# An encoder trunk on one core: the ninth of eleven feed-forward chunks goes from the plain product to the seven-product form in three of four FFNs, split around the first token tile's end

## Chip, core and metric

The kernel runs on 1 core of one Trainium2 chip. What is measured is the device time of one execution in microseconds (us). Five engines work side by side, each through its own list of instructions in order: TensorE (PE, matmuls), VectorE (DVE), ScalarE (ACT), GpSimd (POOL) and SyncE (SP, which issues most DMAs). An engine that needs what another makes waits at a semaphore, and everything behind it in its list waits with it.

## What is computed

Two encoder layers over 256 tokens of width 1024. Each is a macaron block: half a feed-forward network (FFN), a token mixer beside memory attention, half an FFN, each with an RMS norm before and after it.

```python
def swiglu(h, w_gu, w_down):                       # w_gu 1024 x 5632, w_down 2816 x 1024
    g, u = jnp.split(h @ w_gu, 2, axis=-1)
    return (jax.nn.silu(g) * u) @ w_down

for l in range(DEPTH):                             # DEPTH = 2
    ng = norm_gains[l]
    x = x + FFN_RES_WEIGHT * rms_norm(swiglu(rms_norm(x, ng[0]), ffn_w_gu[l, 0], ffn_w_down[l, 0]), ng[1])
    h = rms_norm(x, ng[2])
    ...                                            # l = 0: retention, l = 1: latent attention (MLA)
    x = x + rms_norm(mix, ng[3])
    x = x + FFN_RES_WEIGHT * rms_norm(swiglu(rms_norm(x, ng[4]), ffn_w_gu[l, 1], ffn_w_down[l, 1]), ng[5])
return x
```

There are four FFNs. In the order of time they are called here FFN 1, retention, FFN 2, FFN 3, MLA, FFN 4.

## The kernel before

**Numbers in two halves.** Every matmul is made of three: each operand is split into a high half (`wh`, `zh`, `ah`, cast by ScalarE) and a low half (`wl`, `zl`, `al`, the rest, subtracted by VectorE), and `mm3` adds high x high, low x high and high x low into one PSUM bank (L143 to L145). A `split` therefore always costs one ScalarE and one VectorE instruction of the same size.

**Tiles.** The 256 tokens are two token tiles t = 0, 1 of 128. An FFN walks over 11 chunks c = 0 to 10 of its 2816 inner columns (`FC` = 256 columns each, `C` = 10 is the last). `gu(t, c)` makes gate and up of a chunk (8 blocks of `mm3`, 24 matmuls of 512 columns) into one PSUM bank; `swiglu(t, c)` empties that bank into `a` (ScalarE and VectorE). `a` must be turned before it can be multiplied by the down weights: for chunks 0 to 9 VectorE transposes 32 x 32 blocks (`aT`) and 16 small DMAs (`exchange`, L254) carry the blocks to their places (`ag`); for chunk 10 TensorE transposes it (`tr`).

**Down product, plain.** `down(t, c)` takes 12 matmuls for one token tile, 24 for both.

**Down product, seven-product form.** For chunks below `fast`, `load_fast`, `take_fast` and `down_fast` do both token tiles at once with seven products instead of eight, each of three matmuls (21 in place of 24). Sums and differences of weight blocks (`wB`, three subtractions, five splits) and of activation blocks (`sr`, four additions, three splits) are made for it on VectorE and ScalarE. The seven products accumulate over the chunks in seven PSUM banks (`prod`), and `combine` adds four of them on VectorE into what belongs to all outputs. PSUM has eight banks of 512 f32 columns in this kernel; while the seven products run, one is left for `gu`, `tr` and everything else. `fast` is 5 in FFN 1 and 8 in FFNs 2, 3 and 4.

**Order.** TensorE's list is written out by hand (`manual_schedule`): in the loop over chunks it alternates `gu(0, c)`, half of a seven-product chunk, `gu(1, c)`, the other half. ScalarE's and VectorE's lists, which buffer a tile gets, and the DMAs' order are made by a scheduler from the program, except inside `in_order()` (the first `post`). The end of an FFN is what the change touches: `gu(0, 10)`, the rest of chunks 6 and 7, `combine`, `tr(0, 10)`, the first half of `gu(1, 10)`, `down(0, 8)`, `down(0, 9)`, `down(0, 10)`, the second half of `gu(1, 10)`, then `post(0)` (norm and residual of token tile 0, and the next stage's `z`), `down(1, 8)`, `tr(1, 10)`, the rest of token tile 1, `post(1)`.

The small buffers: `k1` tiles of 256 f32 columns (12 of them), `e` tiles of 512 (5), split weights `wh` and `wl` (9 each), raw weights (5).

Of the kernel before, what the change touches and what calls it, by code (L numbers as in the profile page):

```python
# [31 lines left out]
def kernel(ctx, tc, x, mem, positions, norm_gains, ffn_w_gu, ffn_w_down, w_o,  # L32
                        mem_norm, mem_w_kv, ret_w_in, ret_log_decay, ret_head_norm,
                        mla_w_in, mla_q_norm, mla_kv_norm, mla_w_uq, mla_w_ukv, inv_freq, out):
    nc = tc.nc
    V, S, G, T = nc.vector, nc.scalar, nc.gpsimd, nc.tensor
# [4 lines left out]
    wk = ctx.enter_context(tc.tile_pool(name="wk", bufs=2))  # L41
# [5 lines left out]
    def in_order():  # L47

        return tc.manual_schedule(engines={mybir.EngineType.Activation, mybir.EngineType.DVE})
# [3 lines left out]
        return wk.tile([P, n], dt, name=name, tag="t2", bufs=9)  # L53

    def k1(name, n=256, dt=F32):
        return wk.tile([P, n], dt, name=name, tag="k1", bufs=12)

    def esm(name):
        return wk.tile([P, 512], F32, name=name, tag="e", bufs=5)

    def bank():
        return ps.tile([P, 512], F32, name="bank", tag="bank")
# [199 lines left out]
    def ffn(l, j, zs, gains, extra=(), first=None, fast=0):  # L262
# [5 lines left out]
        sums, prod, gu_last = [[None, None], [None, None]], [], {}  # L268
        extra = dict(extra)
        C = NFC - 1  # L270

        def load_gu(c):
            gu_w[c] = [weights(gu_src(wgu, c, u), 1024) for u in range(KB // 2)]
            gu_last[c] = last_load[0]

        def load_d(c):
            d_w[c] = [weights(wd[c * FC + b * P:c * FC + (b + 1) * P, :], 1024) for b in range(2)]
# [64 lines left out]
                T.matmul(out=prod[p], lhsT=al if x == 2 else ah, rhs=bl if x == 1 else bh,  # L342
                         start=c == 0 and x == 0, stop=x == 2 and c == fast - 1 and not own)

        def combine():

            m1, m5, m7, m6 = prod[0], prod[2], prod[3], prod[6]
            c1, u, v, w = esm("c1"), esm("u"), esm("v"), esm("w")
            S.copy(out=c1, in_=m1)
            add = lambda o, a, b: V.tensor_tensor(out=o, in0=a, in1=b, op=ALU.add)  # L350
            add(u, m6, c1)
            add(v, m5, u)
            add(u, m7, u)
            add(w, m5, u)
            sums[:] = [[c1, v], [u, w]]

        def gu(t, c, part=None):
            if c not in gu_w:
                load_gu(c)
            for k in range(KB) if part is None else range(part * 4, part * 4 + 4):  # L360
                gu_k(t, c, k)
            if part is None:
                swiglu(t, c)

        def gu_k(t, c, k):
# [64 lines left out]
        def down(t, c, hs=(0, 1)):  # L430
            if c not in d_w:
                load_d(c)
            ah, al = at[t, c]
            for i in hs:
                new = accs[t][i] is None
                if new:
                    accs[t][i] = bank()
                for b in range(2):
                    wh, wl = d_w[c][b]
                    n = slice(i * 512, (i + 1) * 512)  # L440
                    m = slice(b * P, (b + 1) * P)
                    mm3(accs[t][i], ah[:, m], al[:, m], wh[:, n], wl[:, n],
                        new and b == 0, c == NFC - 1 and b == 1)
# [5 lines left out]
        def half(c, h):  # L449
            if 0 <= c < fast:  # L450
                down_fast(c, *(range(11, 21) if h else range(11)))
                if h and c == fast - 1:
                    combine()

        if first:
            gu_w[0] = first.w
# [43 lines left out]
            both(C - 3)  # L500
        tr(0, C)
        gu(1, C, 0)
        down(0, C - 2)
        down(0, C - 1)
        down(0, C)
        gu(1, C, 1)
        with in_order():
            z0 = post(0, accs[0], gain_post, True, next_gain, lambda: swiglu(1, C), sums[0])
        down(1, C - 2)
        tr(1, C)  # L510
        down(1, C - 1)
        down(1, C, (0,))
# [719 lines left out]
    zs = [Z(), Z()]  # L1232
# [82 lines left out]
    def mem_extra(m):  # L1315
# [7 lines left out]
        def third():  # L1323
# [6 lines left out]
    late = {7: lambda: (late_mem[7](), angles.append(rope_angles())), 8: lambda: (late_mem[8](), tables()),  # L1330
            9: lambda: (late_mem[9](), tables2())}
    zs = ffn(0, 0, zs, lambda: (gpost(0, 1), gpre(0, 2)), late, first=First(), fast=5)
    zs = retention(zs, m0, lambda: (gpost(0, 3), gpre(0, 4)))
    zs = ffn(0, 1, zs, lambda: (gpost(0, 5), gpre(1, 0)), fast=8)
    m1 = Mem(1, m0.kept)
    zs = ffn(1, 0, zs, lambda: (gpost(1, 1), gpre(1, 2)), {c: lambda i=c - 5: m1.fetch(i) for c in range(5, 9)}, fast=8)
    zs = mla(zs, m1, lambda: (gpost(1, 3), gpre(1, 4)))
    ffn(1, 1, zs, lambda: (gpost(1, 5), None), fast=8)


_INS = ['x', 'mem', 'positions', 'norm_gains', 'ffn_w_gu', 'ffn_w_down', 'w_o', 'mem_norm', 'mem_w_kv',
# [31 lines left out]
```

## Time and profile before

| | us |
|---|---|
| median of 3 runs (lowest to highest) | 945.88 (945.87 to 946.54) |
| the profiled execution's own time | 946.14 |
| its span, first to last instruction | 944.4 |
| PE busy in the span | 929.0 (98%) |
| DVE busy | 787.0 (83%) |
| ACT busy | 589.4 (62%) |

The profile follows one execution. Matmuls are pipelined, so that a matmul's own duration (0.39 us) is longer than the distance to the next one (0.23 us for 512 columns). Where TensorE loses time is read from start to start, and from the waits named behind a row.

### The profile page before, as it was taken

What the parts mean: (1) busy time and instruction counts of PE and PEld (TensorE: products, weight loads), DVE (VectorE), ACT (ScalarE), POOL (GpSimd) and SP (SyncE); (2) the same over time, 40 slices, a digit from 0 to 9 for tenths busy, and PEclk for the clock granted to TensorE, in tenths of its full rate; (3) what the DMA queues carried; (4) which work ended last, traced back from release to release, by engine and by line L of the source; (5) the groups of instructions that cost most, each with busy time, mean ns of one, the idle gap of its engine ahead of it and who ended that gap; (6) DMA issues with size and microseconds to landing.
All of it is one profiled execution on the core that took longest, in us unless ns stands there. A gap on an engine that the chain in (4) does not pass through costs nothing.

```text
span 944.4 us, 13761 instructions
## 1 busy us (share of the span) xinstructions
PE 929.0 (98%) x4400; PEld 772.0 (82%) x4400; DVE 787.0 (83%) x1341; ACT 589.4 (62%) x1030; POOL 179.0 (19%) x328
## 2 busy tenths in 40 slices
PE   9999999999999999999999999999999999999996
PEld 7878878898888888888887878888897888888885
DVE  6989979587886788999988699999766887999994
ACT  7656665456665565666656467676568864666761
POOL 0331231030000114033101332031020013330210
PEclk9999999999999999999999999999999999999998
DMA  9966478684655575767457967855551759667531
GB/s 314 336 219 217 142 239 268 207 278 140 198 170 182 153 257 195 247 223 239 144 158 224 326 196 240 264 184 192 169 187 44 246 157 301 190 199 236 170 133 45
DMA packets 152537, 194.25 MB, mean 206 GB/s; under 512 B 15112, under 2 KB 126224, under 8 KB 152464
## 3 DMA queue, kind: packets, MB, share of 16 engines
q1 hardware_dynamic: 143232, 183.92, 60.4%
q0 software_dynamic: 9216, 9.46, 3.3%
q8 instruction: 34, 0.56, 0.2%
q14 instruction: 39, 0.32, 0.1%
q10 hardware_dynamic: 16, 0.00, 0.0%
HBM read 179.69 MB, written 3.15 MB: 194 GB/s over the span
## 4 chain that ended last, share of the span: by engine, by line
PE 81%; DMA 7%; DVE 5%; ACT 3%; issue 2%; POOL 1%; SPq 1%; DVEq 0%; POOLq 0%; ACTq 0%
PE bank L145 21%; PE bank L143 21%; PE bank L144 21%; PE bank L342 14%; DMA raw<-in_ffn_w_gu_dram 3%; DMA ag<-aT 3%; PE bank L173 2%; DVE wl L77 2%; ACT wh L76 1%; POOL ag L254 1%; PE bank L643 1%; PE bank L898 1%; DVE x L241 1%; PE bank L884 1%; ACT e L654 0%
## 5 line engine op out<-in xcount | busy, mean ns | idle before, releaser
L143 PE MATMUL bank<-wh,zh 128*128 128x512 f32 (+2 forms) x944 | 364.6, 386 | 0.0
L144 PE MATMUL bank<-wl,zh 128*128 128x512 f32 (+2 forms) x944 | 360.5, 382 | 1.1 <-DVE wl L77 1.1
L145 PE MATMUL bank<-wh,zl 128*128 128x512 f32 (+2 forms) x944 | 360.5, 382 | 0.4 <-DVE zl L77 0.4
L77 DVE TENSOR_TENSOR wl<-raw,wh 128x1024 fp32r<-128x1024 f32 (+2 forms) x262 | 311.1, 1210 | 34.7 <-ACT wh L76 32.0
L76 ACT CAST wh<-raw 128x1024 fp32r<-128x1024 f32 (+2 forms) x262 | 269.8, 1045 | 65.3 <-PE bank L145 19.4
L254 POOL DMA_DIRECT2D ag<-aT x288 | 141.3, 498 | 393.3 <-ACT sh L76 280.1
L144 PEld LDWEIGHTS bank<-wl,zh 128*128 128x128 f32 x944 | 177.9, 188 | 35.2 <-DVE wl L77 1.8
L145 PEld LDWEIGHTS bank<-wh,zl 128*128 128x128 f32 x944 | 177.5, 188 | 35.3 <-DVE zl L77 1.0
L143 PEld LDWEIGHTS bank<-wh,zh 128*128 128x128 f32 x944 | 177.8, 188 | 33.4 <-issue 0.7
L76 ACT CAST wh<-wB 128x1024 fp32r<-128x1024 f32 (+1 forms) x116 | 94.4, 836 | 75.0 <-DVE wB L297 39.5
L77 DVE TENSOR_TENSOR wl<-wB,wh 128x1024 fp32r<-128x1024 f32 (+1 forms) x116 | 108.0, 952 | 11.6 <-ACT wh L76 10.4
L377 ACT ACTIVATE s<-bank,rstd 128x256 f32<-128x256 f32 x88 | 41.6, 472 | 48.3 <-PE bank L145 44.8
L143 PE MATMUL bank<-wh,ah 128*128 128x512 f32 x120 | 47.6, 396 | 0.0
L148 POOL TENSOR_TENSOR prs<-ms,nhalf 128x1 f32<-128x1 f32 x12 | 10.1, 843 | 194.0 <-DVE ms L161 194.0
L145 PE MATMUL bank<-wh,al 128*128 128x512 f32 x120 | 46.9, 390 | 0.0
L144 PE MATMUL bank<-wl,ah 128*128 128x512 f32 x120 | 46.7, 390 | 0.0
L76 ACT CAST ah<-ag 128x256 fp32r<-128x256 f32 x80 | 25.2, 368 | 18.1 <-DMA ag<-aT 16.0
L401 DVE STREAM_TRANSPOSE aT<-a 128x256 f32<-128x256 f32 x80 | 35.4, 443 | 0.9
L148 POOL TENSOR_TENSOR rstd<-ms,nhalf 128x1 f32<-128x1 f32 x14 | 21.2, 1518 | 78.6 <-DVE ms L161 78.6
L342 PE MATMUL bank<-wh,sl 128*128 128x512 f32 x87 | 34.6, 398 | 1.4 <-DVE sl L77 1.4
L76 ACT CAST sh<-sr 128x512 fp32r<-128x512 f32 x29 | 18.0, 621 | 28.2 <-DVE sr L318 28.2
L342 PE MATMUL bank<-wh,sh 128*128 128x512 f32 x87 | 34.5, 397 | 1.0 <-ACT sh L76 1.0
(213 smaller groups left out, 1164.1 us busy)
## 6 DMA issues: line engine op xcount, KB each, us to landing
raw<-in_ffn_w_gu_dram SPq DMA_DIRECT2D x352, 256.0 KB, 4.6
raw<-in_ffn_w_down_dram SPq DMA_DIRECT2D x30, 512.0 KB, 4.8
wB<-in_ffn_w_down_dram SPq DMA_DIRECT2D x58, 256.0 KB, 4.6
wB<-in_ffn_w_down_dram SPq DMA_DIRECT2D x29, 512.0 KB, 4.0
raw<-in_ret_w_in_dram SPq DMA_DIRECT2D x48, 256.0 KB, 4.1
ag<-aT POOLq DMA_DIRECT2D x288, 32.0 KB, 3.6
raw<-in_w_o_dram SPq DMA_DIRECT2D x16, 512.0 KB, 4.0
raw<-in_mem_w_kv_dram SPq DMA_DIRECT2D x8, 512.0 KB, 5.4
```

The lines of the kernel that those rows point to most:

```text
L76: ins = S.copy(out=hi, in_=src).ins
L77: V.tensor_tensor(out=lo, in0=src, in1=hi.bitcast(F32), op=ALU.subtract)
L143: T.matmul(out=dst, lhsT=ah, rhs=bh, start=start, stop=False)
L144: T.matmul(out=dst, lhsT=ah, rhs=bl, start=False, stop=False)
L145: T.matmul(out=dst, lhsT=al, rhs=bh, start=False, stop=stop)
L148: G.tensor_tensor(out=dst, in0=src, in1=nhalf.broadcast_to(list(src.shape)), op=ALU.pow)
L173: T.transpose(out=tp[:s.shape[1], j * P:(j + 1) * P], in_=s, identity=ident)
L241: V.scalar_tensor_tensor(out=xx[:, sl], in0=y[i][:, sl], scalar=r, in1=xx[:, sl], op0=ALU.mult, op1=ALU.add)
L254: queues[q % len(queues)].dma_start(out=g[q * 32:(q + 1) * 32, i * 256:(i + 1) * 256], in_=b[sl, q * 256:(q + 1) * 256])
L342: T.matmul(out=prod[p], lhsT=al if x == 2 else ah, rhs=bl if x == 1 else bh, start=c == 0 and x == 0, stop=x == 2 and c == fast - 1 and no ...
L377: s_ins = S.activation(out=s, in_=p[:, 0:FC], func=AF.Silu, scale=z.r).ins
L401: V.transpose(out=b.rearrange("p (q u t b x) -> p u t q b x", q=4, u=2, t=2, b=2)[:, c % 2, t], in_=act.pop((t, c)).rearrange("p (b q x) - ...
```

## The change

In FFNs 2, 3 and 4 `fast` becomes 9, so that chunk 8 is made with seven products. Its 21 matmuls are not done in one go: products 0, 6, 2, 4 and 1 (15 matmuls), which token tile 0 needs, stand where `down(0, 8)` (12) stood, and products 3 and 5 (6 matmuls) where `down(1, 8)` (12) stood. `combine` is cut in two, one part behind each. GpSimd's space for DMA descriptors goes from 1024 to 2048 bytes per partition, and `k1` gives up one of its 12 buffers for it. FFN 1 keeps its form.

```diff
-        return wk.tile([P, n], dt, name=name, tag="k1", bufs=12)
+        return wk.tile([P, n], dt, name=name, tag="k1", bufs=11)
...
-        def combine():
+        def add(o, a, b):
+            V.tensor_tensor(out=o, in0=a, in1=b, op=ALU.add)
+
+        def combine(t):
             m1, m5, m7, m6 = prod[0], prod[2], prod[3], prod[6]
-            c1, u, v, w = esm("c1"), esm("u"), esm("v"), esm("w")
-            S.copy(out=c1, in_=m1)
-            add = lambda o, a, b: V.tensor_tensor(out=o, in0=a, in1=b, op=ALU.add)
-            add(u, m6, c1)
-            add(v, m5, u)
-            add(u, m7, u)
-            add(w, m5, u)
-            sums[:] = [[c1, v], [u, w]]
+            if t == 0:
+                c, u, v = esm("c"), esm("u"), esm("v")
+                S.copy(out=c, in_=m1)
+                add(u, m6, c)
+                add(v, m5, u)
+                sums[:] = [[c, v], [u, esm("w")]]
+            else:
+                u, w = sums[1]
+                add(u, m7, u)
+                add(w, m5, u)
...
                 if h and c == fast - 1:
-                    combine()
+                    combine(0)
+                    combine(1)
...
         tr(0, C)
         gu(1, C, 0)
-        down(0, C - 2)
+        late = C - 2 == fast - 1
+        if late:
+            down_fast(C - 2, *(3 * p + x for p in (0, 6, 2, 4, 1) for x in range(3)))
+            combine(0)
+        else:
+            down(0, C - 2)
         down(0, C - 1)
         down(0, C)
         gu(1, C, 1)
+        if late:
+            down_fast(C - 2, *(3 * p + x for p in (3, 5) for x in range(3)))
         with in_order():
             z0 = post(0, accs[0], gain_post, True, next_gain, lambda: swiglu(1, C), sums[0])
-        down(1, C - 2)
+        if late:
+            combine(1)
+        else:
+            down(1, C - 2)
         tr(1, C)
...
-    zs = ffn(0, 1, zs, lambda: (gpost(0, 5), gpre(1, 0)), fast=8)
+    zs = ffn(0, 1, zs, lambda: (gpost(0, 5), gpre(1, 0)), fast=9)
...
-    nc = _bacc.Bacc("TRN2", target_bir_lowering=False, num_devices=1, dynamic_dma_scratch_size=1024)
+    nc = _bacc.Bacc("TRN2", target_bir_lowering=False, num_devices=1, dynamic_dma_scratch_size=2048)
```

Three places in the engines' lists, all of FFN 2's end. The number behind a name tells buffers apart.

TensorE, before: the end of chunk 7 (L342), the two transposes of `tr(0, 10)` into `bank_5031`, and the start of the first half of `gu(1, 10)` into `bank_5036`; in brackets the engine whose semaphore a row waits for.

```order
L342 MATMUL bank_3898<-wTh_4984,sl_4826 128x512
L173 MATMUL bank_5031<-ident_77,a_4947 128x128 [waits PE_49]
L173 MATMUL bank_5031<-ident_77,a_4947 128x128
L143 MATMUL bank_5036<-wh_4895,zh_3523 128x512 [waits Activation_49]
L144 MATMUL bank_5036<-wl_4896,zh_3523 128x512
L145 MATMUL bank_5036<-wh_4895,zl_3524 128x512
```

The same rows after the change.

```order
L342 MATMUL bank_3898<-wTh_4993,sl_4826 128x512
L173 MATMUL bank_5031<-ident_77,a_4947 128x128 [waits PE_49]
L173 MATMUL bank_5031<-ident_77,a_4947 128x128
L143 MATMUL bank_5036<-wh_4895,zh_3523 128x512 [waits DVE_49]
L144 MATMUL bank_5036<-wl_4896,zh_3523 128x512
L145 MATMUL bank_5036<-wh_4895,zl_3524 128x512
```

Nothing moved here, but the fourth row waited for ScalarE before and waits for VectorE now.

VectorE, before: from the first split of chunk 8's weights (`wl_5052`) to `al_5030`, the row that reads `tr(0, 10)`'s bank last. `al_4952` and `al_4958` are chunks 8 and 9, `wl_4983` is chunk 7.

```order
L77 TENSOR_TENSOR wl_5052<-raw_5049,wh_5051 128x1024
L77 TENSOR_TENSOR al_4952<-ag_4838,ah_4951 128x256 x2
L77 TENSOR_TENSOR wl_4983<-wB21_4974,wh_4982 128x512
L77 TENSOR_TENSOR wl_5058<-raw_5055,wh_5057 128x1024
L77 TENSOR_TENSOR al_4958<-ag_4838,ah_4957 128x256 x2
L77 TENSOR_TENSOR wl_5076<-raw_5073,wh_5075 128x1024
L350 TENSOR_TENSOR u_5021<-bank_3898,c1_5020 128x512
L77 TENSOR_TENSOR wl_5082<-raw_5079,wh_5081 128x1024
L350 TENSOR_TENSOR v_5022<-bank_3894,u_5021 128x512
L77 TENSOR_TENSOR al_5030<-bank_5031,ah_5029 128x256
```

The same stretch after the change; three additions of 128 columns into `sr_4953`, which read the `ag` of chunks 8 and 9 too, stand ahead of its first row.

```order
L77 TENSOR_TENSOR wl_5055<-wB_5049,wh_5054 128x1024
L318 TENSOR_TENSOR sr_4953<-ag_4838,sr_4953 128x128
L77 TENSOR_TENSOR al_4952<-ag_4838,ah_4951 128x256
L77 TENSOR_TENSOR al_4952<-ag_4838,ah_4951 128x128
L77 TENSOR_TENSOR wl_4992<-wB21_4983,wh_4991 128x512
L77 TENSOR_TENSOR sl_4955<-sr_4953,sh_4954 128x512
L297 TENSOR_TENSOR wB_5049<-wB_5049 128x1024
L77 TENSOR_TENSOR al_4967<-ag_4838,ah_4966 128x256 x2
L300 TENSOR_TENSOR wB_5049<-wB_5049 128x512
L77 TENSOR_TENSOR wl_5057<-wB_5049,wh_5056 128x1024
L77 TENSOR_TENSOR al_5030<-bank_5031,ah_5029 128x256
```

The first row of the stretch stood ahead of everything that reads `ag` before; now it stands behind three rows that do. The weights of chunk 9 (`wl_5076`, `wl_5082`) and the first sums of `combine` stood ahead of `al_5030` and have gone behind it; the sums and splits of chunk 8 have come ahead of it.

VectorE, before: the splits of the four weight tiles of the next FFN's first chunk (`wl_5255`, `wl_5262`, `wl_5269`, `wl_5276`), and the first rows of `post(1)` (`u_5021`, `w_5023`). `al_5175` is `tr(1, 10)`, `zl_5200` the next FFN's first `z`.

```order
L77 TENSOR_TENSOR wl_5255<-raw_5251,wh_5254 128x1024
L77 TENSOR_TENSOR al_5175<-bank_5176,ah_5174 128x256
L77 TENSOR_TENSOR wl_5262<-raw_5258,wh_5261 128x1024
L77 TENSOR_TENSOR wl_5269<-raw_5265,wh_5268 128x1024
L77 TENSOR_TENSOR wl_5276<-raw_5272,wh_5275 128x1024
L226 TENSOR_TENSOR u_5021<-bank_3897,u_5021 128x512
L77 TENSOR_TENSOR zl_5200<-bank_5201,zh_5199 128x512
L77 TENSOR_TENSOR zl_5200<-bank_5208,zh_5199 128x512
L226 TENSOR_TENSOR w_5023<-bank_5167,w_5023 128x512
```

After the change; `combine(1)`'s two sums and the row of `tr(1, 10)` stand just ahead of these, and `wl_5275`, `wl_5282`, `wl_5289` are the first three weight tiles.

```order
L77 TENSOR_TENSOR wl_5275<-raw_5271,wh_5274 128x1024
L77 TENSOR_TENSOR wl_5282<-raw_5278,wh_5281 128x1024
L77 TENSOR_TENSOR zl_5220<-bank_5221,zh_5219 128x512
L77 TENSOR_TENSOR zl_5220<-bank_5228,zh_5219 128x512
L226 TENSOR_TENSOR u_5091<-bank_3897,u_5091 128x512
L226 TENSOR_TENSOR w_5096<-bank_5206,w_5096 128x512
L222 TENSOR_TENSOR y_5241<-u_5091,gpost_4013 128x512
L222 TENSOR_TENSOR y_5242<-w_5096,gpost_4013 128x512
L161 SCALAR_TENSOR_TENSOR ms_5252<-ss_5247 128x1
L77 TENSOR_TENSOR wl_5289<-raw_5285,wh_5288 128x1024
L241 SCALAR_TENSOR_TENSOR x1_80<-y_5241,prs_5254,x1_80 128x512
L241 SCALAR_TENSOR_TENSOR x1_80<-y_5242,prs_5254,x1_80 128x512
```

All four stood ahead of `post(1)` before. Now two do; the third stands behind its sums, and the fourth (`wl_5296`) behind two more rows of 512 columns (`z`) and a tiny one (`ms`) that follow here.

## Rows read from the trace of the kernel before

**Rows 1.** The page, busy time by engine: us, share, instructions.

```profile
PE 929.0 (98%) x4400; PEld 772.0 (82%) x4400; DVE 787.0 (83%) x1341; ACT 589.4 (62%) x1030; POOL 179.0 (19%) x328
```

**Rows 2.** Timeline of PE, FFN 2's end: start, us, engine, line, what, [idle].

```profile
474.94 0.38 PE L173 MATMUL bank<-ident,a 128*128 128x128 f32 x2
475.08 0.48 PE L143 MATMUL bank<-wh,zh 128*128 128x512 f32 x1
...
486.07 0.39 PE L143 MATMUL bank<-wh,zh 128*128 128x512 f32 x1
...
498.14 0.39 PE L143 MATMUL bank<-wh,zh 128*128 128x512 f32 x1
...
505.06 0.50 PE L144 MATMUL bank<-wl,zh 128*128 128x512 f32 x1 [1.10 <-DVE wl L77]
```

**Rows 3.** Timeline of PE, ends of FFN 3 and 4, start of MLA.

```profile
655.52 0.48 PE L143 MATMUL bank<-wh,zh 128*128 128x512 f32 x1
...
678.58 0.28 PE L143 MATMUL bank<-zh,wh 128*128 128x256 f32 x1
...
684.33 0.35 PE L143 MATMUL bank<-wh,zh 128*128 128x416 f32 x1
...
914.34 0.48 PE L143 MATMUL bank<-wh,zh 128*128 128x512 f32 x1
```

**Rows 4.** Timeline of DVE, chunk 7's seven-product work in FFN 2.

```profile
462.61 0.43 DVE L77 TENSOR_TENSOR al<-ag,ah 128x256 fp32r<-128x256 f32 x1
462.94 0.29 DVE L318 TENSOR_TENSOR sr<-ag,sr 128x128 f32<-128x128 f32 x1
463.14 0.29 DVE L77 TENSOR_TENSOR al<-ag,ah 128x128 fp32r<-128x128 f32 x1
...
463.71 1.19 DVE L297 TENSOR_TENSOR wB<-wB 128x1024 f32<-128x1024 f32 x1
464.81 0.69 DVE L77 TENSOR_TENSOR sl<-sr,sh 128x512 fp32r<-128x512 f32 x1
465.41 0.69 DVE L300 TENSOR_TENSOR wB<-wB 128x512 f32<-128x512 f32 x1
466.08 1.83 DVE L77 TENSOR_TENSOR wl<-wB,wh 128x1024 fp32r<-128x1024 f32 x2
```

**Rows 5.** Timeline of ACT, first row that reads chunks 8 and 9, FFN 2, 3, 4.

```profile
470.76 0.71 ACT L76 CAST ah<-ag 128x256 fp32r<-128x256 f32 x2 [0.87 <-DMA ag<-aT]
...
651.01 0.71 ACT L76 CAST ah<-ag 128x256 fp32r<-128x256 f32 x2 [0.69 <-DMA ag<-aT]
...
910.92 0.71 ACT L76 CAST ah<-ag 128x256 fp32r<-128x256 f32 x2 [1.87 <-DMA ag<-aT]
```

**Rows 6.** Timeline of DVE, post(0) and tr(1, 10) in FFN 2.

```profile
489.97 0.74 DVE L241 SCALAR_TENSOR_TENSOR x<-y,prs,x 128x512 f32<-128x512 f32 x1
490.63 1.29 DVE L197 TENSOR_TENSOR z<-x,gpre 128x512 f32<-128x512 f32 x2
491.84 1.22 DVE L77 TENSOR_TENSOR wl<-raw,wh 128x1024 fp32r<-128x1024 f32 x1
492.97 0.42 DVE L77 TENSOR_TENSOR al<-bank,ah 128x256 fp32r<-128x256 f32 x1
```

**Rows 7.** Windows around the first chunk of FFN 1 and FFN 3: busy us, PEclk, DMA share.

```profile
51.00:55.20 4.20, 2.81 (x11) 1.21 (x9) 3.55 (x10) 3.58 (x6) 0.00 (x0) 0.98 0.59 216
55.50:58.60 3.10, 3.10 (x8) 2.42 (x8) 3.10 (x7) 0.95 (x4) 0.00 (x0) 0.52 0.73 186
543.50:548.00 4.50, 3.12 (x11) 1.51 (x10) 4.00 (x10) 4.02 (x7) 0.00 (x0) 1.00 0.02 7
```

**Rows 8.** Timeline of POOL, the first exchange of FFN 1 and of FFN 3.

```profile
36.93 4.09 POOL L254 DMA_DIRECT2D ag<-aT  x8 [8.22 <-DVE aT L401]
43.54 3.90 POOL L254 DMA_DIRECT2D ag<-aT  x8 [2.52 <-DMA ag<-aT]
...
535.45 4.03 POOL L254 DMA_DIRECT2D ag<-aT  x8 [4.13 <-DMA ag<-aT]
```

More of the change, by code (lines that the diff above doesn't have):

```diff
@@ L1333 @@
     zs = retention(zs, m0, lambda: (gpost(0, 3), gpre(0, 4)))
-    zs = ffn(0, 1, zs, lambda: (gpost(0, 5), gpre(1, 0)), fast=8)
+    zs = ffn(0, 1, zs, lambda: (gpost(0, 5), gpre(1, 0)), fast=9)
     m1 = Mem(1, m0.kept)
-    zs = ffn(1, 0, zs, lambda: (gpost(1, 1), gpre(1, 2)), {c: lambda i=c - 5: m1.fetch(i) for c in range(5, 9)}, fast=8)
+    zs = ffn(1, 0, zs, lambda: (gpost(1, 1), gpre(1, 2)), {c: lambda i=c - 5: m1.fetch(i) for c in range(5, 9)}, fast=9)
     zs = mla(zs, m1, lambda: (gpost(1, 3), gpre(1, 4)))
-    ffn(1, 1, zs, lambda: (gpost(1, 5), None), fast=8)
+    ffn(1, 1, zs, lambda: (gpost(1, 5), None), fast=9)
 _INS = ['x', 'mem', 'positions', 'norm_gains', 'ffn_w_gu', 'ffn_w_down', 'w_o', 'mem_norm', 'mem_w_kv',
```

## Prediction

> **What bounds the kernel.** I read the page's busy times first. PE is busy in 929.0 of 944.4 us, the next engine in 787.0 [rows 1]: the time is that of PE's list, and any other engine counts only where PE waits for it. Then I read PE's timeline at the ends of the FFNs, from start to start. From the start of the first half of `gu(1, 10)` (475.08) to that of its second half (486.07) stand 48 matmuls of 512 columns, 0.229 us each [rows 2]. This stretch has no gap that a wait is named for: `tr(0, 10)` starts at 474.94, and the next matmul follows its two transposes 0.14 us after. The only wait at the border to FFN 3 is 1.10 us for a weight split (505.06). Last I read what VectorE and ScalarE do in these stretches [rows 4 to 6], because the change gives them work and takes little from PE.
>
> **What is removed.** Chunk 8 takes 21 matmuls in place of 24, in three FFNs: 9 matmuls of 0.229 us, or 2.06 us.
>
> **The wait that is added, and why.** Before, PE emptied a bank early: `combine` began before `tr(0, 10)`, and `gu(1, 10)` could write to the bank of product 0 as soon as ScalarE had copied it; that is the semaphore of ScalarE in the first order piece. Now all seven banks of products stay held until chunk 8 has added to them, and chunk 8 stands behind `gu(1, 10)`. Eight banks less seven is one: `tr(0, 10)` and `gu(1, 10)` must share it. `gu(1, 10)` therefore waits until VectorE has read the transposes (`al_5030`); that is the semaphore of VectorE in the second piece. Behind the waiting matmul stands all of PE's list.
>
> How long, is VectorE's list ahead of `al_5030`. It can't go past the first `sr` before the exchange of chunks 8 and 9 has landed. ScalarE's first reader of `ag` shows when that is: 470.76, 651.01, 910.92 [rows 5]. From there, start to start in [rows 4, 6]: three `sr` 0.60; `wl` 1.13; `sr` 0.20; `al` 0.33 and 0.20; `wl` of 512 columns 0.60 (as `sl`); `sl` 0.60; `wB` of 1024 1.10; two `al` 0.66; `wB` of 512 0.67; `wl` 1.13; together 7.22. `al_5030` itself takes 0.42, a semaphore about 0.05: 7.7 us. ScalarE's share is ready earlier: its last row of these starts behind `wB` of 1024 and its rows are no longer than VectorE's. So `gu(1, 10)` can start at 478.46, 658.71 and 918.62 in place of 475.08, 655.52 and 914.34 [rows 2, 3]: 3.38, 3.19 and 4.28, **10.85 us in all**. The floor is what the turn costs with VectorE idle: in `tr(1, 10)` `al` ends 1.87 us after its transposes started at about 491.5 (492.97 plus 0.42) [rows 6], of which some 0.35 was queue; 1.4 us a time, 4.2 in all. I take 10.85, since the list ahead of the row is known.
>
> **Work that costs nothing.** Behind `al_5030` stand 8.2 us of VectorE's rows up to chunk 10's last weights (six of 512 columns, four of 1024, by the same durations); beside them PE has 12 + 15 + 24 matmuls, 11.7 us. Without that cover they would cost up to 8.2 us a time. Chunk 8's weights leave HBM ahead of the exchange or just behind it, where the stage's DMAs had room. `tr(1, 10)` has only 6 matmuls ahead of it where 12 stood; its `a` was ready just before 489.97, 3.9 us after `gu`'s second half began, and is wanted after 18 matmuls, 4.12: nothing, or 0.2 in one FFN. One `k1` buffer less and the 2 KB: neither engine's list changes in retention or in GpSimd's queue, so I take nothing; at worst a VectorE row of 0.4 us waits at one matmul group, a few tenths.
>
> **What is late next.** Let T be the start of `gu(1, 10)`'s second half (486.07). Before, the next FFN began at 498.14, T + 12.07 [rows 2]; with 6 matmuls less it begins at T + 10.70. VectorE ends `post(0)`'s `z` at 491.84, T + 5.77 [rows 6]. Behind it stand now (third order place) `u`, `al`, `w`, two `wl`, two `zl`, `u`, `w`, two `y`, `ms`: 0.60 + 0.33 + 0.60 + 2.26 + 1.20 + 1.20 + 1.20 + 0.1, to T + 13.26; the third weight tile's low half is ready at T + 14.48. PE wants it 13 matmuls in, at T + 13.68: 0.8 us. The fourth stands behind two `x` (0.66 each), two `z` (1.21) and `ms`: ready at T + 18.2, wanted six matmuls after the third, T + 15.85: 2.4 us. The 1.10 us wait of before falls away, since the next tile's split follows at once. Together +2.1 us at FFN 3's start. At MLA's start the same rows are pushed back, but 5.75 us of key matmuls stand first (678.58 to 684.33) [rows 3]: between 0 and 2.1; I take 0.5, nearer to nothing because of that cover. FFN 4 has no next stage.
>
> **The clock.** A stretch of 4.20 us in which PE was busy for 2.81 was followed by one with a granted clock of 0.52 (the lower level, 1.2 of 2.4 GHz): 3.10 us, which lose 1.5 us. In FFN 3, 4.50 us with 3.12 busy were not: 1.00 [rows 7]. The new wait is 3 us with nothing at all, emptier than either, so I count one lower stretch in each of three FFNs, 4.5 us; the bounds are 0 and five (FFN 3's and MLA's start too), 7.5. The Trainium skill (TensorE: Matmul & The Clock Gate, section Why this matters for your kernels) says that a gap between matmul bursts puts the clock back to its lower state. By that rule the sum is 961.8; by the third window of rows 7 alone, where gaps did not, 957.3. The trace has agreed once and disagreed once.
>
> **Sum.** −2.06 + 10.85 + 2.1 + 0.5 + 4.5 = +15.9. The profiled execution took 946.14 us (span 944.4), so 962.0; the median of the runs is 0.26 lower: **961.8 us**.
>
> **Rivals.**
> - *The clock stays up* (chance 0.28): the waits without 4.5, 957.3. For it: FFN 3's first chunk; against it, the length of the gap.
> - *The wait is hidden* (0.06 wholly, 0.03 down to about 0.7 us a time), the other side: `gu(1, 10)` gets a bank of its own, PE keeps its 2.06 and VectorE's extra work lies beside it: 943.8. It decides at 0.69 us of wait a time (2.06 / 3). Against it: the floor above is twice that even with VectorE idle, and the semaphore moved from ScalarE to VectorE.
> - *Descriptor space pays* (0.06): in FFN 1's first exchange GpSimd issues 8 DMAs and waits 2.52 us for one to land, in FFN 3's 4.13 [rows 8]. If the space of 1024 were why, 2048 would end PE's gaps of rows 7, at most 1.4 us each in the two windows, and the low clock of one, 1.5: 957.5 with the waits. Against it: eight were in flight in 1024, and GpSimd's list is the same.
> - *The splits at the next stages cost more, or the clock falls five times* (0.07): up to 966.4, from the terms' upper ends below.
>
> **Chances.** My forecast as it stands has 0.50. Faster by over 0.2% (1.9 us, about what a measurement of this kernel tells from no change) is the wholly hidden wait, 0.06; within 0.2% the one hidden down to 0.7 us, 0.03; all else is slower, 0.91. The low end is the wait and the saving alone, 945.88 + 10.85 − 2.06 = 954.7; the high end adds 2.1 at both next stages and five low stretches, 966.4. Range 954.5 to 966.5.
>
> **What would show it.** Right: in three FFNs, PE idle for about 3 us (4 in FFN 4) between `tr(0, 10)` and the next matmul, released by VectorE's `al`; 9 matmuls less; two new waits for `wl` in FFN 3's first chunk, and 505.06's gone; a granted clock near 0.5 behind the three gaps. Wrong: the matmul behind `tr(0, 10)` starts 0.14 us after it, as before; or `al_5030` comes much earlier than 7.7 us after the exchange has landed; or the clock reads 1.00 behind the gaps.

## The result, and the profile after

| | before | after |
|---|---|---|
| median of 4 runs (lowest to highest), us | 946.21 (945.87 to 948.49) | 962.19 (962.08 to 962.32) |
| ratio, with its 95% interval | | 1.0166 (1.015 to 1.0183) |
| the profiled execution, its span, us | 946.14, 944.4 | 962.21, 960.4 |

The kernel became slower by 16.0 us. 961.8 was predicted.

The page's line of busy times, the one that answers to [rows 1]:

```profile
PE 931.7 (97%) x4391; PEld 772.2 (80%) x4391; DVE 802.0 (84%) x1374; ACT 597.4 (62%) x1042; POOL 183.0 (19%) x328
```

PE has its 9 matmuls less, and VectorE 15 us more to do: 802.0 for 787.0.

PE's waits by line and releaser in the kernel after (us in total, times, longest):

```profile
PE bank L143 <- DVE al L77: 8.5, 3, 2.8
PE bank L144 <- DVE wl L77: 5.2, 4, 2.6
...
PE bank L342 <- DVE wl L77: 1.0, 1, 1.0
```

The first line is new: the first matmul of `gu(1, 10)` waits for VectorE's `al`, once in each of three FFNs. The second answers to the 1.10 us at 505.06 in [rows 2], which was its only case; now there are four.

PE's timeline after, at the places of [rows 2, 3]:

```profile
474.17 0.38 PE L173 MATMUL bank<-ident,a 128*128 128x128 f32 x2
477.38 0.50 PE L143 MATMUL bank<-wh,zh 128*128 128x512 f32 x1 [2.83 <-DVE al L77]
...
490.70 0.39 PE L143 MATMUL bank<-wh,zh 128*128 128x512 f32 x1
...
494.78 0.40 PE L173 MATMUL bank<-ident,a 128*128 128x128 f32 x2
...
505.33 0.50 PE L144 MATMUL bank<-wl,zh 128*128 128x512 f32 x1 [0.84 <-DVE wl L77]
...
509.59 0.80 PE L144 MATMUL bank<-wl,zh 128*128 128x512 f32 x1 [2.61 <-DVE wl L77]
...
661.16 0.38 PE L173 MATMUL bank<-ident,a 128*128 128x128 f32 x2
664.37 0.50 PE L143 MATMUL bank<-wh,zh 128*128 128x512 f32 x1 [2.82 <-DVE al L77]
...
676.06 0.39 PE L143 MATMUL bank<-wh,zh 128*128 128x512 f32 x1
...
695.58 0.46 PE L144 MATMUL bank<-wl,zh 128*128 128x416 f32 x1 [0.35 <-DVE wl L77]
...
704.95 0.38 PE L144 MATMUL bank<-wl,zh 128*128 128x256 f32 x1 [1.45 <-DVE wl L77]
...
925.00 0.50 PE L342 MATMUL bank<-wl,ah 128*128 128x512 f32 x1 [1.00 <-DVE wl L77]
...
926.27 0.38 PE L173 MATMUL bank<-ident,a 128*128 128x128 f32 x2
929.48 0.79 PE L143 MATMUL bank<-wh,zh 128*128 128x512 f32 x1 [2.84 <-DVE al L77]
```

Read the distance from the transposes (L173) to the row below them: 3.21 us three times, of which two transposes are about 0.11; so PE stands empty for 3.10 us at each end. In FFN 2 the same two rows stood 0.14 us apart before [rows 2], so that 3.07 us are lost each time. The named wait (2.83) is shorter than the loss, since the last transpose's own run and the release are not counted in it. By the same start-to-start reading FFN 4 loses another 1.15 us ahead of its transposes (925.00), FFN 3's start 1.00 and 2.77 (505.33, 509.59), and MLA's start 0.52 and 1.62 (695.58, 704.95).

VectorE's timeline in FFN 2, from the first row that reads chunks 8 and 9 to the row that frees the bank:

```profile
469.67 0.29 DVE L315 TENSOR_TENSOR sr<-ag 128x128 f32<-128x128 f32 x1 [1.35 <-DMA ag<-aT]
...
475.77 1.22 DVE L77 TENSOR_TENSOR wl<-wB,wh 128x1024 fp32r<-128x1024 f32 x1
476.91 0.41 DVE L77 TENSOR_TENSOR al<-bank,ah 128x256 fp32r<-128x256 f32 x1
```

VectorE never pauses between 469.67 and 477.32: 7.65 us, where the prediction added up 7.7.

The same last row in the kernel before:

```profile
478.49 0.41 DVE L77 TENSOR_TENSOR al<-bank,ah 128x256 fp32r<-128x256 f32 x1
```

It ended at 478.90, 3.96 us after `tr(0, 10)` had started (474.94). After the change it ends 3.15 us after that start (474.17 to 477.32). VectorE thus reads the transposes no later than before; what is new is that a matmul wants their bank.

Windows of the same kernel behind three of the gaps, and around FFN 1's first chunk (us, then busy us of PE, PEld, DVE, ACT and POOL, then the granted clock of TensorE, DMA share, GB/s):

```profile
51.70:55.90 4.20, 2.33 (x8) 0.83 (x6) 3.60 (x10) 3.62 (x6) 0.00 (x0) 1.00 0.45 172
55.90:59.00 3.10, 3.10 (x14) 2.52 (x15) 3.10 (x7) 1.22 (x4) 0.00 (x0) 1.00 0.63 178
...
478.70:482.10 3.40, 3.40 (x10) 2.58 (x10) 3.30 (x4) 1.81 (x4) 0.00 (x0) 0.54 0.10 15
...
664.40:668.60 4.20, 4.20 (x19) 3.47 (x20) 4.20 (x6) 4.00 (x6) 0.00 (x0) 1.00 0.07 7
509.50:512.80 3.30, 3.21 (x8) 2.61 (x9) 2.35 (x4) 1.25 (x2) 2.72 (x1) 0.54 0.47 152
929.40:933.00 3.60, 3.52 (x10) 2.81 (x11) 3.60 (x6) 2.12 (x3) 0.00 (x0) 0.59 0.00 0
```

A granted clock near 0.5 stands behind FFN 2's gap (478.7), FFN 4's (929.4) and the one at FFN 3's start (509.5). Behind FFN 3's own gap, which is as long to 0.01 us, it is 1.00 (664.4). FFN 1's first chunk, which was followed by a low clock before [rows 7], keeps the full clock here, although PE was busy for less of it: 2.33 of 4.20 us, 2.81 before.

**What a lower stretch costs** can be read without a model. From `gu(1, 10)`'s first half to its second stand 51 matmuls: 11.69 us in FFN 3 (664.37 to 676.06) and 13.32 in FFN 2 (477.38 to 490.70): 1.63 us.

**The sum of the trace:** 9 matmuls of 0.229 us −2.06; ends of three FFNs 3 × 3.07 + 1.15 = +10.36; FFN 3's start 1.00 + 2.77 − 1.25 (what 505.06 cost before, start to start) = +2.5; MLA's start +2.1; three lower stretches +4.5 (from `tr(0, 10)` to `tr(1, 10)` it is 20.61 us in FFN 2 and 20.45 in FFN 4 for 19.01 in FFN 3, and at FFN 3's start the stretch cost 1.5); up to FFN 1's `tr(1, 10)` (185.05, 186.11 before; its lower stretch is gone) −1.1. FFN 3's first chunk stalls for 0.9 us in place of 2.4, −1.5. That is 14.8 of the 16.0 us by which the spans differ; 1.2 is spread over small pieces.

### The profile page after: what moved, and what is told of

Read it like the earlier page. It is cut to its first block, busy times and chain, and to the rows that moved or that the text cites. A ratio compares the mean times of both kernels' runs of the same rounds, so it can differ in the third digit from the quotient of the medians.

```text
span 960.4 us, 13795 instructions
## 1 busy us (share of the span) xinstructions
PE 931.7 (97%) x4391; PEld 772.2 (80%) x4391; DVE 802.0 (84%) x1374; ACT 597.4 (62%) x1042; POOL 183.0 (19%) x328
## 3 DMA queue, kind: packets, MB, share of 16 engines
HBM read 179.69 MB, written 3.15 MB: 190 GB/s over the span
## 4 chain that ended last, share of the span: by engine, by line
PE 74%; DVE 9%; DMA 7%; ACT 3%; issue 3%; SPq 3%; POOL 2%; DVEq 0%; POOLq 0%; ACTq 0%
PE bank L143 19%; PE bank L145 19%; PE bank L144 19%; PE bank L342 11%; DVE wl L77 3%; DMA ag<-aT 3%; DMA raw<-in_ffn_w_gu_dram 3%; PE bank L173 2%; DMA wB<-in_ffn_w_down_dram 2%; SPq L254 1%; ACT wh L76 1%; PE bank L692 1%; PE bank L660 1%; DVE al L77 1%; POOL ag L254 1%
## 5 line engine op out<-in xcount | busy, mean ns | idle before, releaser
L77 DVE TENSOR_TENSOR wl<-raw,wh 128x1024 fp32r<-128x1024 f32 (+1 forms) x256 | 302.6, 1207 | 32.2 <-ACT wh L76 28.9
L76 ACT CAST wh<-raw 128x1024 fp32r<-128x1024 f32 (+1 forms) x256 | 263.6, 1045 | 69.6 <-PE bank L145 25.1
L76 ACT CAST wh<-wB 128x1024 fp32r<-128x1024 f32 (+1 forms) x128 | 104.2, 835 | 76.9 <-DVE wB L297 41.3
L77 DVE TENSOR_TENSOR wl<-wB,wh 128x1024 fp32r<-128x1024 f32 (+1 forms) x128 | 119.2, 950 | 11.8 <-ACT wh L76 11.1
L342 PE MATMUL bank<-wh,sl 128*128 128x512 f32 x96 | 37.6, 392 | 1.3 <-DVE sl L77 1.3
L342 PE MATMUL bank<-wl,ah 128*128 128x512 f32 x96 | 37.7, 393 | 1.1 <-DVE wl L77 1.0
L297 DVE TENSOR_TENSOR wB<-wB 128x1024 f32<-128x1024 f32 x32 | 38.5, 1202 | 0.1
L143 PE MATMUL bank<-wh,ah 128*128 128x512 f32 x96 | 38.2, 398 | 0.0
L342 PE MATMUL bank<-wh,ah 128*128 128x512 f32 x96 | 37.5, 390 | 0.6 <-ACT ah L76 0.6
L342 PE MATMUL bank<-wh,sh 128*128 128x512 f32 x96 | 37.5, 391 | 0.5 <-ACT sh L76 0.5
L145 PE MATMUL bank<-wh,al 128*128 128x512 f32 x96 | 37.5, 390 | 0.0
```

The lines of the kernel that those rows point to most:

```text
L76: ins = S.copy(out=hi, in_=src).ins
L77: V.tensor_tensor(out=lo, in0=src, in1=hi.bitcast(F32), op=ALU.subtract)
L143: T.matmul(out=dst, lhsT=ah, rhs=bh, start=start, stop=False)
L145: T.matmul(out=dst, lhsT=al, rhs=bh, start=False, stop=stop)
L297: V.tensor_tensor(out=w[:, 0:1024], in0=w[:, 512:1536], in1=w[:, 0:1024], op=ALU.subtract)
```

## The experiments

They ran in four groups on four chips (e1 to e4, e5 to e8, e9 to e11, e12), and there the runs of one kernel spread more widely than in the first comparison: 62 runs of the kernel before, in four groups, have medians of 944.5 to 945.1 and reach from 942.3 to 950.0 us. Differences below 2 us are therefore read from the traces, and times are given as a ratio to the kernel before in the same group.

**e1_space: k1 and the descriptor space alone, on the kernel before.**

```diff
-        return wk.tile([P, n], dt, name=name, tag="k1", bufs=12)
+        return wk.tile([P, n], dt, name=name, tag="k1", bufs=11)
...
-    nc = _bacc.Bacc("TRN2", target_bir_lowering=False, num_devices=1, dynamic_dma_scratch_size=1024)
+    nc = _bacc.Bacc("TRN2", target_bir_lowering=False, num_devices=1, dynamic_dma_scratch_size=2048)
```

> The kernel before with two things of the change alone: one k1 buffer less and 2 KB of descriptor space. Theory: no change, 946.2 within 0.5, GpSimd still pauses about 2.5 us in FFN 1's first exchange and 4.1 us in FFN 3's. Rival (descriptor space pays): the pauses end and so do PE's gaps in the two first chunks, 942 to 945.

Ratio 0.9999 (0.998 to 1.0019): no change. But GpSimd's pause in FFN 3's first exchange was 2.00 us, not 4.1, and PE lost only 0.1 us there. Whether the space did that, this run can't say; the next pair bears on it.

**e6_changed_1kb: the changed kernel with 1024 bytes**, beside **e5_changed_again**, the changed kernel as it is.

```diff
-    nc = _bacc.Bacc("TRN2", target_bir_lowering=False, num_devices=1, dynamic_dma_scratch_size=2048)
+    nc = _bacc.Bacc("TRN2", target_bir_lowering=False, num_devices=1, dynamic_dma_scratch_size=1024)
```

> The changed kernel as it is, beside the others on one chip. Theory: 16 us over the kernel before; waits for al of 2.8 us behind tr(0, 10) three times.

> The changed kernel with the descriptor space back at 1024 bytes. Theory (the space costs and gives nothing): the time of the changed kernel within 1 us. Rival (the space shortens GpSimd's pause in FFN 3's first exchange: 4.1 to 4.2 us in the two profiles with 1024, 2.0 to 3.4 in the four with 2048): the pause is 4 us again, PE's stalls in that chunk grow from under 1 us to 1.7 to 2.4 us, and the time by 1 to 2 us.

e5: ratio 1.0204 (1.0186 to 1.0222), median 962.75; e6: 1.0198 (1.0175 to 1.0221), median 963.31. The space gives nothing that the time shows. GpSimd's timeline of e6, FFN 3's first exchange, its second eight:

```profile
539.08 0.50 POOL L254 DMA_DIRECT2D ag<-aT  x1 [3.18 <-DMA ag<-aT]
```

The pause lies within those of the profiles with 2048 bytes (2.0 to 3.7), below the 4.13 of before [rows 8], and PE's stalls in that chunk were 1.4 us (0.9 in the changed kernel, 2.4 before). In all profiles with five raw buffers the pause is 3.18, 4.13 and 4.22 us with 1024 bytes, and 2.00 to 3.73 with 2048. In e10 it is 0.75 us, with 1024 bytes and a sixth raw buffer. So the space does not set it alone. Against the kernel before, e5 lost 18 us in the median here and 16.0 in the first comparison; the traces show the same waits in both, and where the other 2 us come from stays open.

**e2_ffn4_only: `fast=9` in FFN 4 alone.**

```diff
-    zs = ffn(0, 1, zs, lambda: (gpost(0, 5), gpre(1, 0)), fast=9)
+    zs = ffn(0, 1, zs, lambda: (gpost(0, 5), gpre(1, 0)), fast=8)
...
-    zs = ffn(1, 0, zs, lambda: (gpost(1, 1), gpre(1, 2)), {c: lambda i=c - 5: m1.fetch(i) for c in range(5, 9)}, fast=9)
+    zs = ffn(1, 0, zs, lambda: (gpost(1, 1), gpre(1, 2)), {c: lambda i=c - 5: m1.fetch(i) for c in range(5, 9)}, fast=8)
```

> The change in FFN 4 alone, where no stage follows. Theory: 3 matmuls less (-0.69), the waits for chunk 7's weights (1.15) and for the transposes' bank (3.10) and one lower stretch of the clock (1.5): +5.1 on the kernel before, 951.3. Rival (the clock's fall costs nothing that the time shows): 949.8. Rival (the cost lies in the next stages): within 1 of the kernel before.

Ratio 1.0057 (1.0033 to 1.0081), +5.4 us. The rival that puts the cost into the next stages alone falls: here none follows. Between +5.1 and +3.6, with or without the clock, the time can't decide; in the profiled run the clock did fall, with 20.72 us from `tr(0, 10)` to `tr(1, 10)`. PE's timeline has the two waits:

```profile
912.64 0.50 PE L342 MATMUL bank<-wl,ah 128*128 128x512 f32 x1 [0.79 <-DVE wl L77]
...
917.12 0.50 PE L143 MATMUL bank<-wh,zh 128*128 128x512 f32 x1 [2.84 <-DVE al L77]
```

**e3_gu_first: the bank.** PE's list is written so that no two users want the one free bank.

```diff
-        tr(0, C)
+        if not late:
+            tr(0, C)
         gu(1, C, 0)
...
             combine(0)
+            tr(0, C)
...
```

> The changed kernel, with the first half of gu(1, 10) ahead of tr(0, 10): gu takes the bank that gu(0, 10) left, and tr takes product 0's after the 15 products. Theory (the wait is for a bank): the three waits for al of 3.1 us are gone; VectorE's backlog shows as smaller waits for chunk 8's and chunk 9's weights, about 1.7 us a time; the clock stays up behind them in the two FFNs where it fell: 962.2 - 3 x 1.4 - 3.0 = 955, between 953 and 957. Rival (VectorE's backlog costs the same 3 us wherever it is met): 961 to 963.

Ratio 1.0092 (1.0058 to 1.0125), median 954.29: as the first theory said. PE's waits by line and releaser:

```profile
PE bank L144 <- DVE wl L77: 5.9, 8, 2.6
...
PE bank L342 <- DVE wTl L77: 0.8, 3, 0.3
```

The timeline, from chunk 8's fifteen products to chunk 9:

```profile
478.90 0.50 PE L342 MATMUL bank<-wTl,sh 128*128 128x512 f32 x1 [0.30 <-DVE wTl L77]
...
486.17 0.51 PE L144 MATMUL bank<-wl,ah 128*128 128x512 f32 x1 [0.17 <-DVE wl L77]
```

No wait for `al` is left. VectorE has as many rows to do as in the changed kernel (1374), and PE comes to what they make several times a little early: 0.3 and 0.17 us here. Start to start these small waits add up to about 1.8 us at the ends of FFN 2 and FFN 3 and to 2.6 in FFN 4 (1.0 of it for chunk 7's weights), near the 1.7 that was expected. So of the 3.07 us lost at an end, another order of the same matmuls gives back about 1.3; the rest is VectorE's backlog, met elsewhere. The waits at FFN 3's and MLA's start are unchanged (2.61 is the longest), and a low clock stands behind FFN 3's start alone.

**e4_gap_filled: the clock.** In the gap PE adds zeros to a product bank. The tiles of zeros take room, and the descriptor space goes back to 1024 bytes for them, which by e1 and e6 changes no time.

```diff
         tr(0, C)
         late = C - 2 == fast - 1
+        if late:
+            for i in range(12):
+                T.matmul(out=prod[5], lhsT=zero, rhs=zs[1].h[:, 0:512], start=False, stop=False)
         gu(1, C, 0)
...
-    nc = _bacc.Bacc("TRN2", target_bir_lowering=False, num_devices=1, dynamic_dma_scratch_size=2048)
+    nc = _bacc.Bacc("TRN2", target_bir_lowering=False, num_devices=1, dynamic_dma_scratch_size=1024)
```

> The changed kernel with 12 matmuls that add zeros to a product bank (2.75 us) in the 3.1 us gap behind tr(0, 10); the wait's end stays where it is. Theory (the empty gap lowers the clock, and that costs 1.5 us a time): granted clock near 1 behind the gaps of FFN 2 and FFN 4, 962.2 - 3.0 = 959.2; the lower stretch at FFN 3's start stays. Rival (a lower stretch costs nothing that the time shows): 962.2. Where the fill moved the lower stretch to a later gap instead, the time stays too, but the records show the stretch.

Ratio 1.0158 (1.0121 to 1.0195), median 960.61, 2.1 below e5 with overlapping spreads: alone this proves little. In the profiled run (961.85) the clock stayed up at FFN 3's start, where the expectation had left the fall, and fell to 0.50 behind 2.2 us of stalls in FFN 3's first chunk instead. What the fill does is seen in the trace. PE's timeline around FFN 2's filled gap:

```profile
473.57 0.38 PE L173 MATMUL bank<-ident,a 128*128 128x128 f32 x2
473.70 3.04 PE L512 MATMUL bank<-zh,zero 128*128 128x512 f32 x12
476.79 0.50 PE L143 MATMUL bank<-wh,zh 128*128 128x512 f32 x1
```

The windows view behind it:

```profile
476.80:480.20 3.40, 3.40 (x15) 2.83 (x16) 3.40 (x6) 3.12 (x5) 0.00 (x0) 1.00 0.02 5
```

`gu(1, 10)` starts as late as in the changed kernel, 3.22 us after the transposes, so the wait is VectorE's and not PE's to shorten; but the clock stays up. The distance from `tr(0, 10)` to `tr(1, 10)` is a clean measure of the clock, because nothing but matmuls stands there behind the gap. It is 19.00, 19.02 and 19.14 us in the three FFNs of this run. In the runs with the gap empty it has two values. PE's timeline of e5:

```profile
472.36 0.38 PE L173 MATMUL bank<-ident,a 128*128 128x128 f32 x2
491.39 0.40 PE L173 MATMUL bank<-ident,a 128*128 128x128 f32 x2
656.45 0.38 PE L173 MATMUL bank<-ident,a 128*128 128x128 f32 x2
675.48 0.44 PE L173 MATMUL bank<-ident,a 128*128 128x128 f32 x2
921.69 0.38 PE L173 MATMUL bank<-ident,a 128*128 128x128 f32 x2
942.21 0.44 PE L173 MATMUL bank<-ident,a 128*128 128x128 f32 x2
```

19.03, 19.03 and 20.52: the clock fell in FFN 4 alone. Over the six profiles with empty gaps there are 16 of them, and 10 were followed by a lower clock: all six of FFN 4, two of five in FFN 2, two of five in FFN 3. Nine of the ten took 20.4 to 20.8 us, one (in e7, where the clock stayed low for longer) 22.0; the other six 19.0. So a fall costs 1.4 to 1.8 us as a rule, and how many a run has differs from run to run of one kernel: the profiled run of the first comparison had three and took 962.21, that of e5 had one and took 957.71.

**e7_splits_first: the next stage's splits.** FFN 3's first four weight tiles are split ahead of `post(1)` on VectorE.

```diff
+        after = ()
+        if nxt is not None:
+            nxt.append([weights(gu_src(ffn_w_gu[l + 1, 0], 0, u), 1024) for u in range(KB // 2)])
+            after = (last_lo[0],)
+        with behind(*after):
             z1 = post(1, accs[1], gain_post, True, next_gain, None, sums[1])
...
```

> The changed kernel with FFN 3's first four weight splits ordered ahead of post(1) on VectorE, as they stood before. Theory (VectorE's backlog at the border is what costs, not the order of its rows): the two waits of 1.0 and 2.8 us go, and one of about 3.5 us comes at the next token tile's or the next chunk's weights; the time stays within 1.5 us of the changed kernel. Rival (the order alone is the cause): nothing comes back, and 3.8 us of waits and the lower stretch behind them go, -4 to -5.

Ratio 1.0205 (1.0189 to 1.0221), that of e5. Of the waits at FFN 3's start one is left in PE's timeline, at the next weights:

```profile
512.75 0.50 PE L146 MATMUL bank<-wl,zh 128*128 128x512 f32 x1 [3.34 <-DVE wl L77]
```

3.61 us start to start, for 3.77 before the edit. The order of VectorE's rows is not the cause there; VectorE has too much to do.

**e8_ffn4_reordered and e9_all_reordered: PE's whole end written anew**, in FFN 4 alone (`fast` 8, 8, 9) and in three FFNs (9, 9, 9).

```diff
         if late:
+            gu(1, C, 0)
+            gu(1, C, 1)
+            swiglu(1, C)
             down_fast(C - 2, *(3 * p + x for p in (0, 6, 2, 4, 1) for x in range(3)))
             combine(0)
+            tr(0, C)
+            tr(1, C)
             down_fast(C - 2, *(3 * p + x for p in (3, 5) for x in range(3)))
+            down(0, C - 1)
+            down(0, C)
+            with in_order():
+                z0 = post(0, accs[0], gain_post, True, next_gain, None, sums[0])
             combine(1)
+            down(1, C - 1)
...
```

> Chunk 8 with seven products in FFN 4 alone, and PE's list at its end written so that the bank and VectorE's list have time: both halves of gu(1, 10) first, then the 15 products, both transposes, the other 6 products, chunks 9 and 10. Theory: no wait of over 0.5 us from tr(0, 10) to the end, 3 matmuls less: 0.7 below the kernel before, which these runs can't tell from no change. Rival (chunk 8's work on VectorE costs wherever it is met): 1 to 4 above it.

> PE's list of the run before (both halves of gu(1, 10) first) in all three FFNs with nine seven-product chunks. Theory (VectorE's extra work for chunk 8 has no cover at a border with a next stage): no wait above 0.7 us between tr(0, 10) and the last chunk, but token tile 0's z and the next weights come late: 2.5 to 4 us at the start of FFN 3 and of MLA; -2.06 + 6 = about +4 on the kernel before, 948.5. Rival (the order was the whole cost): 2 us below the kernel before. Rival (nothing is gained by order): the changed kernel's 962.

e8: ratio 0.9997 (0.9985 to 1.001), and no wait from `tr(0, 10)` to the end. But one for chunk 7's weights stands ahead of it, which the kernel before has not; PE's timeline of e8:

```profile
910.92 0.50 PE L342 MATMUL bank<-wl,ah 128*128 128x512 f32 x1 [0.65 <-DVE wl L77]
```

Start to start it is 0.8 us, and it takes back what chunk 8 saves: from FFN 4's second group of `z` transposes to its last matmul PE needs 167.35 us (766.20 to 933.55), 167.21 before (769.05 to 936.26). The order takes the price away where no stage follows, and leaves no gain.

e9: 1.0095 (1.0079 to 1.011), +9 where +4 was expected. PE's timeline of e9 at the starts of FFN 3 and MLA:

```profile
497.97 1.76 PE L173 MATMUL bank<-ident,z 128*128 128x128 f32 x8 [2.89 <-DVE z L197]
...
509.59 0.50 PE L144 MATMUL bank<-wl,zh 128*128 128x512 f32 x1 [1.87 <-DVE wl L77]
...
682.78 1.94 PE L173 MATMUL bank<-ident,z 128*128 128x128 f32 x8 [2.78 <-DVE z L197]
```

The FFNs' ends have no wait above 0.5 us behind `tr(0, 10)`, and the borders have got it: 3.05 and 2.93 us for `z`, behind the first another 2.03 for weights (1.25 in the kernel before), and a lower clock behind both, which the expectation had not counted.

**e10_sixth_raw: why MLA's start waits.**

```diff
-        return wp.tile([P, 1024], F32, name="raw", tag="raw", bufs=5)
+        return wp.tile([P, 1024], F32, name="raw", tag="raw", bufs=6)
...
-        return wk.tile([P, n], dt, name=name, tag="k1", bufs=11)
+        return wk.tile([P, n], dt, name=name, tag="k1", bufs=8)
...
-    nc = _bacc.Bacc("TRN2", target_bir_lowering=False, num_devices=1, dynamic_dma_scratch_size=2048)
+    nc = _bacc.Bacc("TRN2", target_bir_lowering=False, num_devices=1, dynamic_dma_scratch_size=1024)
```

In the changed kernel, ScalarE's timeline ahead of the wait at 704.95 shows a load that lands late (696.17) and the cast for the weights that PE waits for (700.67):

```profile
696.17 1.06 ACT L76 CAST wh<-raw 128x1024 fp32r<-128x1024 f32 x1 [2.78 <-DMA raw<-in_mla_w_in_dram]
...
700.67 1.04 ACT L76 CAST wh<-raw 128x1024 fp32r<-128x1024 f32 x1
```

> The changed kernel with a sixth raw weight buffer; k1 goes from 11 to 8 buffers and the descriptor space to 1024 bytes to make room. Theory (MLA's start waits because a raw buffer that VectorE empties late lets its next load start late): the waits at MLA's start, 0.5 and 1.6 us in the changed kernel, fall to 0.7 or less together; FFN 3's start, where VectorE itself is late, keeps its 1.0 and 2.8, and the three waits for al stay: 1.4 us less, and more where other loads were held back too. Rival (VectorE's rows alone delay MLA): its waits stay at 2.1.

Ratio 1.0147 (1.0127 to 1.0167), by the ratios 5 us below e5, by the medians 3. PE's timeline at MLA's start:

```profile
691.18 0.46 PE L144 MATMUL bank<-wl,zh 128*128 128x416 f32 x1 [0.36 <-DVE wl L77]
...
699.62 0.39 PE L144 MATMUL bank<-wl,zh 128*128 128x256 f32 x1 [0.53 <-DVE wl L77]
```

Start to start 0.53 and 0.69 in place of 0.52 and 1.62: the second wait fell by 0.9 us, the first not at all, and together they are 1.22 where 0.7 or less was expected. The run does not show that the load alone was the cause, because VectorE's list changed with the buffers. VectorE's timeline of the changed kernel, the split that PE waits for at 704.95 and the row ahead of it:

```profile
703.40 0.35 DVE L1048 SCALAR_TENSOR_TENSOR cn<-lat,rkv,gc 128x128 f32<-128x128 f32 x1 [0.57 <-POOL rkv L148]
703.67 1.22 DVE L77 TENSOR_TENSOR wl<-raw,wh 128x1024 fp32r<-128x1024 f32 x1
```

That split in e10:

```profile
698.36 1.22 DVE L77 TENSOR_TENSOR wl<-raw,wh 128x1024 fp32r<-128x1024 f32 x1
```

In the changed kernel ScalarE's half was ready at 701.71, and the split stood behind a row `cn` that waited for GpSimd; in e10 that `cn` stands behind the split, at 700.01. How much of the 0.9 us is the load's and how much the order's stays open.

FFN 3's first chunk gave about 1 us more: from the transposes ahead of it (L173) to `tr(0, 10)` it is 145.28 us, 146.23 in e5, and GpSimd's pause in its first exchange is 0.75 us. FFN 1's first chunk has lost its stalls too (1.9 us in e5), but the profile is only 0.1 us ahead of e5's at FFN 1's `tr(1, 10)`. Where the rest of the difference comes from, the profiles don't show.

**e11_ffn4_sixth_raw and e12_before_sixth_raw: the buffer by itself.** e11 is e8 with the sixth buffer, e12 the kernel before with it (`raw` 6, `k1` 8).

> Chunk 8 with seven products in FFN 4 alone, in the reordered form, with the sixth raw buffer (k1 8, 1024 bytes). Theory: the reordered form by itself gave no change that these runs tell; loads that start earlier shorten the stalls in FFN 1's and FFN 3's first chunks and in retention: 1 to 4 us below the kernel before. Rival (the sixth buffer gives nothing, or k1's three buffers were needed): the time of the kernel before or 1 to 3 above.

> The kernel before with the sixth raw buffer (k1 from 12 to 8), nothing of the change. The run with chunk 8's seven products in FFN 4 and this buffer was 0.37% below the kernel before, the one without the buffer 0.03%. Theory: nearly all of it is the buffer's, by the stalls in FFN 3's first chunk and in retention: 2 to 3 us below the kernel before. Rival (the two need each other): within 1 us of it.

e11: 0.9963 (0.9948 to 0.9977), median 941.18. e12: 0.9961 (0.9948 to 0.9974), median 941.30. Both are faster than the kernels before and after, by the same amount, so that the sixth buffer (with `k1` at 8) is all of it. The 3.8 us of e12 are a little more than its theory's 2 to 3. Windows of e12 that answer to [rows 7], around the first chunks of FFN 1 and FFN 3:

```profile
51.00:55.20 4.20, 3.49 (x15) 2.40 (x14) 4.20 (x8) 3.81 (x7) 0.00 (x0) 1.00 0.71 251
536.50:541.00 4.50, 4.50 (x22) 3.72 (x21) 4.50 (x8) 3.98 (x6) 0.00 (x0) 1.00 0.51 165
```

## Why the prediction was right, point by point

- **Saved matmuls:** −2.06 predicted; 4391 matmuls for 4400, at an unchanged 0.229 us (51 in 11.69): −2.06.
- **The bank wait:** right in cause, and near in size. VectorE's list from the landing of the exchange to `al_5030` is 7.65 us (7.7); the waits are 10.36 us with FFN 4's 1.15 (10.85). e3 shows the cause: the same rows on VectorE, another user for the bank, and the wait for `al` is gone. It shows a limit too: some 1.8 us a time come back as waits for weights, so that the bank alone is worth about 1.3 of the 3.07. In FFN 4 the loss came in two pieces and not in one of 4 us: VectorE's splits already held up chunk 7's product 5 (925.00), and behind `tr(0, 10)` it was 3.07 us as in the other two.
- **FFN 3's start:** +2.1 predicted, +2.5 measured, by the two waits named. The third tile's wait is 1.00 (0.8), the fourth's 2.77 (2.4). In e7, with the splits back ahead of `post(1)`, 3.61 us came at the next weights: the waits belong to VectorE's backlog, not to its order.
- **MLA's start:** mis-sized, 0.5 for 2.1. The step that failed is "I take 0.5, nearer to nothing because of that cover". The 5.75 us of key matmuls did not cover the splits: PE waited 0.52 and 1.62 us for weights behind them. For the second wait the trace shows two things that the prediction did not follow: a load that landed late, and VectorE's split behind a row that waited for GpSimd. e10, which changed both, took 0.9 us of it back; the first wait stayed.
- **The clock:** 4.5 predicted, 4.5 measured, with one of the three places wrong: FFN 3's start had the low clock, and the end of FFN 3 had not. That the sizes agree is luck. "One lower stretch in each of three FFNs" was too sure: behind such gaps it came 10 times in 16. In e4, with the gaps filled, it came behind none of three, and each fall that came cost 1.4 us or more. What decides between the 10 and the 6 stays open; all six gaps of FFN 4 are among the 10, and a wait of 0.7 us or more, start to start, stands 4.5 us ahead of each of these. By the rule of the Trainium skill (TensorE: Matmul & The Clock Gate, section Why this matters for your kernels) such a gap puts the clock back; the traces agree in 10 of 16 cases.
- **Costs taken as nothing:** `k1` and the descriptor space are confirmed by e1 and e6. The low clock of FFN 1 in [rows 7] was not there after (−1.1), and FFN 3's first chunk stalled less (−1.5); neither was foreseen. Together they make up for the 1.6 us that MLA's term was short of and most of the 1.2 in small pieces. That the sum came within 0.1 us of the +15.9 is luck; the mechanism of the largest term is not.

## What to carry to other kernels

Count who holds the scarce buffer at the moment the list changes hands: three matmuls less were bought here with a PSUM bank that stayed occupied for one chunk longer, and the price was not the operation but the whole queue ahead of the row that frees the bank. If an engine off the critical path has a backlog, another order moves the meeting point: reordering the critical engine gave back about half of the loss (e3 and e9, +9 us over the kernel before in place of +18), reordering the engine with the backlog nothing (e7). Where no stage follows, the whole price went, and with it the gain (e8). Look at what a late row holds, too: the one change that paid was a sixth load buffer.

## What the runs showed of the hardware that was not expected

- The granted clock after equal gaps is not the same from run to run: 3.10 us empty, with a lower clock in 10 cases of 16. A stretch with PE busy for 2.33 of 4.20 us kept the full clock, one with 2.81 did not [rows 7].
- The same GpSimd list pauses for its first exchange DMA to land between 0.75 and 4.22 us in FFN 3. With 1024 bytes both ends occur, the times below 1 us only with the sixth raw buffer.
- A sixth raw buffer, paid for with four `k1` buffers (8 for 12), took 0.4% off a kernel whose PE is busy for 98% of its span. What the four cost by themselves no run shows; one less (e1) cost nothing that the times show.
